# First block of two feed-forward stages: token chunk outermost, weights by blocks of 128 columns

## The chip, the cores and the metric

The kernel runs on one NeuronCore of a Trainium2 chip. The time is device microseconds of one launch; of the kernel before there are three runs. The core has five engines that each work through their own list of instructions in order and wait for each other by semaphores: TensorE (PE; its weight loads are listed as PEld), VectorE (DVE), ScalarE (ACT), GpSimd (POOL) and SyncE (SP), the last of which issues only DMAs here. GpSimd issues DMAs too.

## The reference

One decoder layer over 1088 tokens (1024 of a prompt, 64 of 8 samples), 1024 channels, in float32:

```
x = x + 0.5 * swiglu(rmsnorm(x, norm_ffn1), ffn1_w_up, ffn1_w_down)
h = rmsnorm(x, norm_mix);  q, k, v, u, g_a, g_b = split(h @ w_in)
x = x + (sigmoid(g_a) * (attention(q, k, v) @ w_attn_branch)
         + sigmoid(g_b) * (pool(u) @ w_pool_branch)) @ w_out
x = x + 0.5 * swiglu(rmsnorm(x, norm_ffn2), ffn2_w_up, ffn2_w_down)
swiglu(h, w_up, w_down): gate, up = split(h @ w_up);  (silu(gate) * up) @ w_down
```

`w_up` is 1024 x 5632 (2816 gate columns, then 2816 up columns), `w_down` 2816 x 1024. The attention is a dilated window attention in three groups, with a bias per distance and head looked up in a table; the biases are prepared at the start of the kernel.

## The kernel before

**Products.** A product is made of three matmuls in a reduced 32-bit format: each operand is split into a high part (a copy by ScalarE that rounds) and a low part (VectorE's subtraction of it), and `mm3` adds high x high, high x low and low x high in one PSUM bank (L269, L270, L271). `split` does both steps (L215 ScalarE, L216 VectorE). The normed tokens lie as `h_hi` and `h_lo` in SBUF, channels on the partitions, 8 tiles of 128 channels; the tokens are cut into three chunks of 360, 360 and 368 columns (`CH`).

**Norm.** `normed` (L330 on) spreads the tokens' factors over the partitions with a matmul (L334), multiplies on VectorE (L337), copies to `h_hi` on ScalarE (L340) and subtracts to `h_lo`: on GpSimd for every third of the 8 tiles, on VectorE for the others (L341). In the first FFN the tokens are transposed on TensorE beforehand (L465); in the second, `norm` sums the squares first and TensorE adds them up over the partitions.

**FFN.** `ffn` (L344) is called twice (L518 and L1258). It walks over 11 blocks of 256 columns (`j`). For each, `wunit` loads 256 gate or up columns as two raw tiles `wr` of 4 x 256 per partition on SyncE's queue (512 KB each), and splits them into `wh` and `wl` of 128 columns each (two of either, from pool `wp`, three buffers per name). `gate` multiplies one half of 128 columns with one chunk, 24 matmuls into a PSUM tile `psa`, and ScalarE applies silu (L385). `up` does the same for the up columns, VectorE multiplies by the silu (L392), and `split` writes `hh` and `hl`, the operands of the down product (`down`), which runs one block later. In block 0 there is no earlier block: gate and up alternate, half `f` outermost, chunk `c` inside. From block 1 on the six gate products come first, then the down product of the block before, then the six up products. `hh`, `hl` and the pieces `dh`, `dl` of `w_down` lie in the pool `fp`, which `ffn` opens on the right side of SBUF.

**What lies there before.** Two pools, `bp` and `ip`, are open on that side until just before the first `ffn` and hold the raw tokens and the tiles of the biases: the one-hot matrix `oh`, the table `tb`, and `fr`, three buffers of 4 x 448. `biases` (L430) makes four rows sets on TensorE (L438), copies each to `fr` on VectorE (L440), and has GpSimd issue two DMAs: `fr` to `f_scr` in DRAM (L441), and for three of the four sets `fr` 128 times over to `f_rep` in DRAM (L443, 512 rows of 448 values). GpSimd then builds `b_scr` by small DMAs out of `f_scr` (L497 to L506). A first write into memory that a closed pool held waits for what still uses it.

**Order.** The engines' lists are written out by a scheduler that simulates the kernel and orders each engine's instructions by it; an order in the source is a wish, not the order of the list. PSUM has four banks `psa`, and `psb` for the rest; the tiles `tmp` have eight buffers.

Of the kernel before, what the change touches and what calls it, by code (L numbers as in the profile page):

```python
# [11 lines left out]
F32 = mybir.dt.float32  # L12
F32R = mybir.dt.float32r
# [7 lines left out]
P = 128  # L21
D = 1024
KD = D // P
# [5 lines left out]
DFF = 2816  # L29
# [88 lines left out]
def body(ctx, tc, x_prompt, x_sample, c128, c512, c2048, state_pool, rel_bias_table,  # L118
# [14 lines left out]
    wp = ctx.enter_context(tc.tile_pool(name="wp", bufs=3))  # L133
# [9 lines left out]
    def psb():  # L143
        return ps.tile([P, 512], F32, tag="b", name="psb")

    def tmp():
        return tmp_pool[0].tile([P, 368], F32, tag="tmp", name="tmp", bufs=8)
# [40 lines left out]
    def load(out, in_):  # L188
        last_load[0] = nc.sync.dma_start(out=out, in_=in_)
# [5 lines left out]
    for g, w in enumerate(WIN):  # L195
        n = (w - 8) * 512
# [11 lines left out]
    def some_copies(n):  # L208
        for _ in range(min(n, len(copies))):
            o, i = copies.pop()  # L210
            with tc.issue_after(last_load[0].ins):
                nc.sync.dma_start(out=o, in_=i)

    def split(hi, lo, src):
        S.activation(hi, src, AF.Copy)  # L215
        V.tensor_tensor(out=lo, in0=src, in1=hi.bitcast(F32), op=ALU.subtract)  # L216

    def wtiles():

        return [[wp.tile([P, KD, P], F32R, tag=x, name=x) for x in ("wh", "wl")] for _ in range(2)]  # L220

    def wsplit(w, f, sl, raw):
        split(w[f][0][:, sl, :], w[f][1][:, sl, :], raw[:, :, f * P:(f + 1) * P])

    def wunit(src):
        w = wtiles()
        raws = []
        for k0 in range(0, KD, 4):
            raw = wp.tile([P, 4, 256], F32, tag="wr", name="wr", bufs=3)
            load(raw, src[k0 * P:(k0 + 4) * P].rearrange("(k p) n -> p k n", p=P))  # L230
            raws.append((raw, slice(k0, k0 + 4)))
        for f in range(2):
            for raw, sl in raws:
                wsplit(w, f, sl, raw)
        return w
# [23 lines left out]
    def taken():  # L259
        w, job = fetched.pop(0)  # L260
        il.finish(job)
        return w

    def mm3(out, pairs, us=0.0):
        n = len(pairs)
        for i, (lh, ll, rh, rl) in enumerate(pairs):
            if i and us:
                il.advance(us)
            PE.matmul(out, lh, rh, start=i == 0, stop=False)  # L269
            PE.matmul(out, lh, rl, start=False, stop=False)  # L270
            PE.matmul(out, ll, rh, start=False, stop=i == n - 1)  # L271

    def proj(w, half, c, hi, lo, ks=(0, KD)):
        if hi is h_hi:
            il.finish(norms[c])
        c0, n = CH[c]
        o = psa()[:, :n]
        wh, wl = w[half]
        mm3(o, [(wh[:, k, :], wl[:, k, :], hi[:, k, c0:c0 + n], lo[:, k, c0:c0 + n])
                for k in range(*ks)], 0.462)  # L280
        clock_after[0] += 0.462
        return o
# [3 lines left out]
    def go():  # L286
        us, clock_after[0] = clock_after[0], 0.0
        il.advance(us)
# [55 lines left out]
    def ffn(xt, w_up, w_down, ncopy, hook):  # L344
        fctx = ExitStack()
        fp = fctx.enter_context(tc.tile_pool(name="fp", bufs=1, side="right"))

        def down(j, hh, hl, last):
            raws, pcs = [], {}
            for f in range(2):  # L350
                r = fp.tile([P, D], F32, tag="dr", name="dr", bufs=2)
                load(r, w_down[(2 * j + f) * P:(2 * j + f + 1) * P, :])
                raws.append(r)
            some_copies(ncopy)
            for dq in range(4):
                for f in range(2):
                    ph = fp.tile([P, 256], F32R, tag="dh", name="dh", bufs=8)
                    pl = fp.tile([P, 256], F32R, tag="dl", name="dl", bufs=8)
                    split(ph, pl, raws[f][:, dq * 256:(dq + 1) * 256])
                    pcs[dq, f] = (ph, pl)  # L360

            def one(d, c):
                c0, n = CH[c]
                o = psb()[:, :n]
                sl = slice((d % 2) * P, (d % 2 + 1) * P)
                mm3(o, [(pcs[d // 2, f][0][:, sl], pcs[d // 2, f][1][:, sl],
                         hh[:, f, c0:c0 + n], hl[:, f, c0:c0 + n]) for f in range(2)])
                xd = xt[:, d, c0:c0 + n]
                V.scalar_tensor_tensor(out=xd, in0=o, scalar=0.5, in1=xd, op0=ALU.mult, op1=ALU.add)  # L369
                il.advance(0.92)  # L370

            if last:
                for c in range(3):
                    for d in range(KD):
                        one(d, c)
                        hook(c, d)
            else:
                for d in range(KD):
                    for c in range(3):
                        one(d, c)  # L380

        def gate(w, f, c):
            o = proj(w, f, c, h_hi, h_lo)
            t = tmp()[:, :CH[c][1]]
            S.activation(t, o, AF.Silu)  # L385
            go()
            return t

        def up(w, f, c, t, hh, hl):
            c0, n = CH[c]  # L390
            o = proj(w, f, c, h_hi, h_lo)
            V.tensor_tensor(out=t, in0=t, in1=o, op=ALU.mult)  # L392
            split(hh[:, f, c0:c0 + n], hl[:, f, c0:c0 + n], t)
            go()

        prev = None
        for j in range(11):
            wg = wunit(w_up[:, j * 256:(j + 1) * 256])
            sil = {}
            if prev is not None:  # L400
                for f in range(2):
                    for c in range(3):
                        sil[f, c] = gate(wg, f, c)
                down(*prev, False)
            wu = wunit(w_up[:, DFF + j * 256:DFF + (j + 1) * 256])
            hh = fp.tile([P, 2, T], F32R, tag="hh", name="hh")
            hl = fp.tile([P, 2, T], F32R, tag="hl", name="hl")
            if prev is None:
                for f in range(2):
                    for c in range(3):  # L410
                        up(wu, f, c, gate(wg, f, c), hh, hl)
            else:
                for f in range(2):
                    for c in range(3):
                        up(wu, f, c, sil[f, c], hh, hl)
            prev = (j, hh, hl)
        down(*prev, True)
        fctx.close()
# [93 lines left out]
    def hook1(c, d):  # L512
# [3 lines left out]
        norms[c] = il.spawn(norm(xt, c, 1))  # L516

    ffn(xt, ffn1_w_up[0], ffn1_w_down[0], 2, hook1)  # L518
    qctx = ExitStack()
    qp = qctx.enter_context(tc.tile_pool(name="qp", bufs=2, side="right"))  # L520
# [21 lines left out]
    for c, gi in [(c, gi) for i in range(2) for c in range(3) for gi in (2 * i, 2 * i + 1)]:  # L542
            c0, n = CH[c]
# [609 lines left out]
    for i in range(8):  # L1153
        w = taken()
# [25 lines left out]
    for i in range(4):  # L1180
        w = taken()
# [36 lines left out]
    for i in range(4):  # L1218
        w = taken()
# [33 lines left out]
    def hook2(c, d):  # L1253
        emit_outs()
        if d % 2:
            outs.append((c, d - 1))

    ffn(xt, ffn2_w_up[0], ffn2_w_down[0], 2, hook2)  # L1258
    emit_outs()
    some_copies(len(copies))  # L1260
# [36 lines left out]
```

## Time and profile before

| | |
|---|---|
| median of 3 runs | 2554.17 us (2551.82, 2554.17, 2554.18) |
| profiled execution, its own time | 2554.82 us |
| its span | 2553.0 us |
| TensorE busy | 2420.6 us (95%), 14820 matmuls |
| VectorE busy | 1098.7 us (43%) |
| ScalarE busy | 615.9 us (24%) |
| GpSimd busy | 179.1 us (7%) |
| TensorE's granted clock, mean | 0.968 of full |

The profile is of one execution, and all times of its rows are microseconds from the start of the span. A row of the timeline gives the start, the busy time, the engine, the line, the operation, the output and the inputs by their names (without numbers), and how many instructions it merges (x4); in brackets stands how long the engine had been idle, and what released it. TensorE is busy nearly throughout: in the 40 equal slices of 64 us that the page shows, it is below 90% in the first three only (0.7, 0.2 and 0.3).

### The profile page before, as it was taken

Reading aid. Unit: us, or ns where it says so; the run is one execution under the profiler, and the core shown is the slowest. Engines: PE = TensorE matmul, PEld = TensorE weight load, DVE = VectorE, ACT = ScalarE, POOL = GpSimd, SP = SyncE. Lnnn points to the kernel's source line nnn. Section 1 sums busy time; section 2 is a strip of 40 time slices with the busy share of each in tenths; the row PEclk is TensorE's granted clock in tenths of the full one; section 3 lists DMA queues with packets and bytes.
Section 4 is the critical chain, followed back from the end, with each engine's and each line's share of the span. In section 5 each row is a group of like instructions: output and inputs, shape, how many; then the busy total and the mean of one; then the engine's idle time right before and its main releaser. Section 6 shows DMA issues by size and latency. Waiting matters only on the chain.

```text
span 2553.0 us, 35907 instructions
## 1 busy us (share of the span) xinstructions
PE 2420.6 (95%) x14820; PEld 2366.8 (93%) x14820; DVE 1098.7 (43%) x2317; ACT 615.9 (24%) x1436; POOL 179.1 (7%) x304
## 2 busy tenths in 40 slices
PE   7239999999999989999999999998999999999999
PEld 6239999999999989989899979998999999999998
DVE  5014333333333484257668524627333333433334
ACT  4012111111111243343334222213111111111111
POOL 3020000000000040201011210002000000000001
PEclk8669999999999999999999999999999999999999
DMA  4231121122221122347565583621122221221132
GB/s 127 36 88 58 58 71 42 70 83 82 83 83 67 34 81 72 128 159 251 169 192 176 194 279 119 234 101 34 34 83 83 83 83 66 83 83 63 38 124 71
DMA packets 155475, 259.11 MB, mean 101 GB/s; under 512 B 14160, under 2 KB 124432, under 8 KB 154528
## 3 DMA queue, kind: packets, MB, share of 16 engines
q1 hardware_dynamic: 141296, 224.26, 26.6%
q0 software_dynamic: 14016, 32.56, 4.5%
q8 instruction: 116, 1.90, 0.3%
q14 instruction: 47, 0.39, 0.0%
HBM read 225.14 MB, written 76.32 MB: 118 GB/s over the span
## 4 chain that ended last, share of the span: by engine, by line
PE 83%; DMA 6%; issue 5%; DVE 3%; POOL 1%; ACT 1%; SPq 0%; POOLq 0%; DVEq 0%; ACTq 0%
PE psa L269 20%; PE psa L270 20%; PE psa L271 20%; PE psb L270 7%; PE psb L271 7%; PE psb L269 7%; DMA f_rep<-fr 2%; DMA b_scr<-f_scr 2%; DMA qb<-q_scr 1%; DMA u_scr<-us 1%; PE psb L864 1%; PE psb L730 1%; DMA wr<-in_ffn_w_up_dram 1%; DMA rt<-u_scr 0%; PE psb L1050 0%
## 5 line engine op out<-in xcount | busy, mean ns | idle before, releaser
L269 PE MATMUL psa<-h_hi,wh 128*128 128x360 f32 (+1 forms) x3216 | 1072.2, 334 | 67.2 <-DVE tmp L392 59.0
L270 PE MATMUL psa<-h_lo,wh 128*128 128x360 f32 (+1 forms) x3216 | 1070.8, 333 | 35.4 <-POOL h_lo L341 27.1
L271 PE MATMUL psa<-h_hi,wl 128*128 128x360 f32 (+1 forms) x3216 | 1065.1, 331 | 0.0
L269 PEld LDWEIGHTS psa<-h_hi,wh 128*128 128x128 f32 x3216 | 613.0, 191 | 79.3 <-DVE tmp L392 59.6
L270 PEld LDWEIGHTS psa<-h_lo,wh 128*128 128x128 f32 x3216 | 613.8, 191 | 43.2 <-POOL h_lo L341 27.4
L271 PEld LDWEIGHTS psa<-h_hi,wl 128*128 128x128 f32 x3216 | 613.4, 191 | 4.5 <-issue 3.6
L216 DVE TENSOR_TENSOR wl<-wr,wh 128x512 fp32r<-128x512 f32 (+1 forms) x284 | 185.4, 680 | 554.7 <-ACT wh L215 554.4
L369 DVE SCALAR_TENSOR_TENSOR xt<-psb,xt 128x360 f32<-128x360 f32 (+1 forms) x528 | 281.5, 533 | 261.6 <-PE psb L271 261.2
L270 PE MATMUL psb<-hl,dh 128*128 128x360 f32 (+1 forms) x1056 | 347.4, 329 | 0.0
L269 PE MATMUL psb<-hh,dh 128*128 128x360 f32 (+1 forms) x1056 | 347.3, 329 | 0.0
L271 PE MATMUL psb<-hh,dl 128*128 128x360 f32 (+1 forms) x1056 | 346.6, 328 | 0.0
L215 ACT ACTIVATE wh<-wr 128x512 fp32r<-128x512 f32 (+1 forms) x284 | 163.2, 618 | 457.7 <-PE psa L270 397.4
L269 PEld LDWEIGHTS psb<-hh,dh 128*128 128x128 f32 x1056 | 198.8, 188 | 0.3
L271 PEld LDWEIGHTS psb<-hh,dl 128*128 128x128 f32 x1056 | 198.5, 188 | 0.0
L270 PEld LDWEIGHTS psb<-hl,dh 128*128 128x128 f32 x1056 | 198.4, 188 | 0.2
L215 ACT ACTIVATE dh<-dr 128x256 fp32r<-128x256 f32 x176 | 72.3, 417 | 499.3 <-PE psb L270 486.5
L392 DVE TENSOR_TENSOR tmp<-tmp,psa 128x360 f32<-128x360 f32 x132 | 69.9, 530 | 211.2 <-PE psa L271 211.2
L215 ACT ACTIVATE hh<-tmp 128x360 fp32r<-128x360 f32 x132 | 65.6, 499 | 238.6 <-DVE tmp L392 198.3
L385 ACT ACTIVATE tmp<-psa 128x360 f32<-128x360 f32 x132 | 61.2, 466 | 233.6 <-PE psa L271 233.5
L216 DVE TENSOR_TENSOR hl<-tmp,hh 128x360 fp32r<-128x360 f32 x132 | 70.0, 532 | 76.0 <-ACT hh L215 75.9
L216 DVE TENSOR_TENSOR dl<-dr,dh 128x256 fp32r<-128x256 f32 x176 | 73.1, 420 | 24.9 <-ACT dh L215 21.9
L889 DVE TENSOR_TENSOR qb<-kt,qb 128x512 f32<-128x512 f32 x96 | 65.4, 684 | 30.9 <-DMA qb<-q_scr 30.2
(239 smaller groups left out, 1520.3 us busy)
## 6 DMA issues: line engine op xcount, KB each, us to landing
wr<-in_ffn_w_up_dram SPq DMA_DIRECT2D x88, 512.0 KB, 4.9
out_dram<-in_cache_kv_w_dram SPq DMA_DIRECT2D x32, 1020.0 KB, 9.4
qb<-q_scr SPq DMA_DIRECT2D x96, 256.0 KB, 4.6
dr<-in_ffn_w_down_dram SPq DMA_DIRECT2D x44, 512.0 KB, 4.2
wr<-in_w_in_dram SPq DMA_DIRECT2D x38, 512.0 KB, 4.7
kt<-in_cache_kv_w_dram SPq DMA_DIRECT2D x64, 256.0 KB, 4.3
vt<-in_cache_kv_w_dram SPq DMA_DIRECT2D x26, 512.0 KB, 8.6
t<-t_scr SPq DMA_DIRECT2D x16, 544.0 KB, 4.7
```

The source lines that it names most:

```text
L215: S.activation(hi, src, AF.Copy)
L216: V.tensor_tensor(out=lo, in0=src, in1=hi.bitcast(F32), op=ALU.subtract)
L269: PE.matmul(out, lh, rh, start=i == 0, stop=False)
L270: PE.matmul(out, lh, rl, start=False, stop=False)
L271: PE.matmul(out, ll, rh, start=False, stop=i == n - 1)
L369: V.scalar_tensor_tensor(out=xd, in0=o, scalar=0.5, in1=xd, op0=ALU.mult, op1=ALU.add)
L385: S.activation(t, o, AF.Silu)
L392: V.tensor_tensor(out=t, in0=t, in1=o, op=ALU.mult)
L730: PE.matmul(o[:rows, 4 * t + 2 * f:4 * t + 2 * f + 2], sqs[f][:, t * P:t * P + rows], halves, start=True, stop=True)
L864: PE.matmul(o[:, h * 64:(h + 1) * 64], pts[i][:, h * P:(h + 1) * P], vs[:, k, h * 64:(h + 1) * 64], start=i == 0, stop=i == len(kt) - 1)
L889: V.tensor_tensor(out=qb, in0=kt.to_broadcast([P, 2, 256]) if g == 0 else kt, in1=qb, op=ALU.mult))
```

## The change

Only the first block (`j` = 0) of both calls of `ffn` is edited. Its weights are now loaded by `wblock`: 128 columns in one raw tile of 8 x 128 per partition (as large as the former tile of 4 x 256, with rows of 512 bytes in DRAM in place of 1024), split in two steps into one pair `wh`, `wl`. The chunk is the outer loop and the half the inner one, so that chunk 0 goes through both halves before chunk 1 is touched. The first halves of gate and up are loaded at the start, the second ones when the loop first comes to them. Three of the four blocks lie in `wp`; the last (the up weights of the second half) lies in `fp`, beside `hh` and `hl`.

```diff
--- before.py
+++ after.py
@@ -393,21 +393,35 @@
             split(hh[:, f, c0:c0 + n], hl[:, f, c0:c0 + n], t)
             go()
 
+        def wblock(c0, pool):
+
+            w = [pool.tile([P, KD, P], F32R, tag=x, name=x) for x in ("wh", "wl")]
+            raw = wp.tile([P, KD, P], F32, tag="wr", name="wr", bufs=3)
+            load(raw, w_up[:, c0:c0 + P].rearrange("(k p) n -> p k n", p=P))
+            for k0 in range(0, KD, 4):
+                split(w[0][:, k0:k0 + 4, :], w[1][:, k0:k0 + 4, :], raw[:, k0:k0 + 4, :])
+            return w
+
         prev = None
         for j in range(11):
-            wg = wunit(w_up[:, j * 256:(j + 1) * 256])
             sil = {}
-            if prev is not None:
+            if prev is None:
+                wg, wu = [wblock(0, wp)], [wblock(DFF, wp)]
+            else:
+                wg = wunit(w_up[:, j * 256:(j + 1) * 256])
                 for f in range(2):
                     for c in range(3):
                         sil[f, c] = gate(wg, f, c)
                 down(*prev, False)
-            wu = wunit(w_up[:, DFF + j * 256:DFF + (j + 1) * 256])
+                wu = wunit(w_up[:, DFF + j * 256:DFF + (j + 1) * 256])
             hh = fp.tile([P, 2, T], F32R, tag="hh", name="hh")
             hl = fp.tile([P, 2, T], F32R, tag="hl", name="hl")
             if prev is None:
-                for f in range(2):
-                    for c in range(3):
+                for c in range(3):
+                    for f in range(2):
+                        if len(wg) == f:
+                            wg.append(wblock(P, wp))
+                            wu.append(wblock(DFF + P, fp))
                         up(wu, f, c, gate(wg, f, c), hh, hl)
             else:
                 for f in range(2):
```

The scheduler turns this into other lists. The first piece is ScalarE's list around the first write of `hh` in the first FFN (L385 silu, L340 `h_hi`, L215 `split`), of before:

```order
L385 ACTIVATE tmp<-psa 128x360
L340 ACTIVATE h_hi<-tmp 128x368 x4
L385 ACTIVATE tmp<-psa 128x360
L215 ACTIVATE wh<-wr 128x512 x2
L385 ACTIVATE tmp<-psa 128x368
L385 ACTIVATE tmp<-psa 128x360
L215 ACTIVATE wh<-wr 128x512 x2
L385 ACTIVATE tmp<-psa 128x360
L215 ACTIVATE hh<-tmp 128x360 x2
```

and of the changed kernel:

```order
L385 ACTIVATE tmp<-psa 128x360
L340 ACTIVATE h_hi<-tmp 128x368 x4
L385 ACTIVATE tmp<-psa 128x360
L215 ACTIVATE hh<-tmp 128x360
L215 ACTIVATE wh<-wr 128x512 x2
L215 ACTIVATE dh<-dr 128x256 x8
L215 ACTIVATE hh<-tmp 128x360
L385 ACTIVATE tmp<-psa 128x360
L215 ACTIVATE hh<-tmp 128x360
```

From here to the first `hh` there stood five silu activations and four weight splits; now there are two activations, and the next weight split stands behind that `hh`.

The second piece is GpSimd's list around the bias copies in the first FFN, of before:

```order
L441 DMA f_scr<-fr 4x448
L443 DMA f_rep<-fr 512x1x448
L341 TENSOR_TENSOR h_lo<-tmp,h_hi 128x368
L502 DMA b_scr<-f_scr 8x4x128 x8
L505 DMA b_scr<-f_scr 32x1x8 x4
L341 TENSOR_TENSOR h_lo<-tmp,h_hi 128x368
L441 DMA f_scr<-fr 4x448
L443 DMA f_rep<-fr 512x1x448
L441 DMA f_scr<-fr 4x448 x2
L443 DMA f_rep<-fr 512x1x448
```

and of the changed kernel, whose L455, L457, L516 and L519 are the former L441, L443, L502 and L505:

```order
L455 DMA f_scr<-fr 4x448
L457 DMA f_rep<-fr 512x1x448
L455 DMA f_scr<-fr 4x448
L457 DMA f_rep<-fr 512x1x448
L341 TENSOR_TENSOR h_lo<-tmp,h_hi 128x368
L516 DMA b_scr<-f_scr 8x4x128 x8
L519 DMA b_scr<-f_scr 32x1x8 x2
L341 TENSOR_TENSOR h_lo<-tmp,h_hi 128x368
L455 DMA f_scr<-fr 4x448
L519 DMA b_scr<-f_scr 32x1x8 x2
L455 DMA f_scr<-fr 4x448
L457 DMA f_rep<-fr 512x1x448
```

The second `f_rep` copy stood behind twelve `b_scr` copies and now stands in front of them, with one `f_scr` copy between it and the first.

The third piece is TensorE's list of the first FFN behind the last of the four bias matmuls. `psa_609` takes the up product of the second half with chunk 0, with weights `wh_574` from `fp`; `psa_637` is the gate of chunk 1. Of the changed kernel:

```order
L452 MATMUL psb_438<-oh_116,tb_115 4x448
L269 MATMUL psa_609<-h_hi_91,wh_574 128x360
L270 MATMUL psa_609<-h_lo_92,wh_574 128x360
L269 MATMUL psa_637<-h_hi_91,wh_493 128x360
L270 MATMUL psa_637<-h_lo_92,wh_493 128x360
L271 MATMUL psa_637<-h_hi_91,wl_494 128x360
```

and of before, where `psa_582` and `psa_609` are gate and up of the first half with chunk 1, both with weights from `wp`:

```order
L438 MATMUL psb_438<-oh_116,tb_115 4x448
L271 MATMUL psa_582<-h_hi_91,wl_494 128x360
L269 MATMUL psa_582<-h_hi_91,wh_493 128x360
L270 MATMUL psa_582<-h_lo_92,wh_493 128x360
L271 MATMUL psa_582<-h_hi_91,wl_494 128x360
L270 MATMUL psa_609<-h_lo_92,wh_509 128x360
```

Three products of chunk 0 are over where the changed list begins, and the fourth is spread between those of chunk 1.

The fourth piece is TensorE's list in the second FFN around the matmul that spreads chunk 1's factors (L334). Of before, where `psa_15142` is the up product of the first half with chunk 0, and `psa_15191` and `psa_15252` are gate and up of chunk 1:

```order
L269 MATMUL psa_15142<-h_hi_91,wh_15063 128x360
L270 MATMUL psa_15142<-h_lo_92,wh_15063 128x360
L271 MATMUL psa_15142<-h_hi_91,wl_15064 128x360
L334 MATMUL psb_15103<-tmp_15001,ones_78 128x360
L269 MATMUL psa_15191<-h_hi_91,wh_15047 128x360
L269 MATMUL psa_15252<-h_hi_91,wh_15063 128x360
L270 MATMUL psa_15191<-h_lo_92,wh_15047 128x360
L271 MATMUL psa_15191<-h_hi_91,wl_15048 128x360
```

and of the changed kernel, where `psa_15126` is the up product of the first half with chunk 0, and `psa_15191` is the gate of the second half with chunk 0:

```order
L269 MATMUL psa_15126<-h_hi_91,wh_15055 128x360
L270 MATMUL psa_15126<-h_lo_92,wh_15055 128x360
L271 MATMUL psa_15126<-h_hi_91,wl_15056 128x360
L334 MATMUL psb_15087<-tmp_15001,ones_78 128x360
L269 MATMUL psa_15126<-h_hi_91,wh_15055 128x360
L270 MATMUL psa_15126<-h_lo_92,wh_15055 128x360
L271 MATMUL psa_15126<-h_hi_91,wl_15056 128x360
L270 MATMUL psa_15191<-h_lo_92,wh_15175 128x360
L271 MATMUL psa_15191<-h_hi_91,wl_15176 128x360
L269 MATMUL psa_15191<-h_hi_91,wh_15175 128x360
```

Behind L334 there stood products of chunk 1; now there stand products of chunk 0.

## Rows read from the trace of the kernel before

**Rows 1.** Busy time by stretch: ends, length, busy us (instructions), clock, DMA share, GB/s

```profile
core 0: us, PE busy (x) PEld busy (x) DVE busy (x) ACT busy (x) POOL busy (x), PEclk, DMA share, GB/s
45.95:86.00 40.05, 16.96 (x95) 15.12 (x93) 5.49 (x11) 3.82 (x7) 5.93 (x9) 0.75 0.26 27
176.96:250.00 73.04, 73.00 (x426) 72.71 (x427) 33.40 (x67) 18.97 (x43) 9.03 (x17) 0.97 0.31 104
250.00:900.00 650.00, 650.00 (x3938) 650.00 (x3937) 245.41 (x482) 124.11 (x262) 2.33 (x3) 1.00 0.19 66
900.00:1700.00 800.00, 781.16 (x5003) 741.60 (x5002) 434.10 (x953) 266.31 (x700) 107.20 (x196) 0.97 0.52 170
1745.00:1750.00 5.00, 3.75 (x20) 2.87 (x18) 4.59 (x16) 1.25 (x4) 1.71 (x2) 1.00 0.00 0
1750.00:1755.00 5.00, 2.47 (x8) 2.17 (x9) 5.00 (x10) 2.65 (x6) 1.49 (x3) 0.71 0.00 0
```

**Rows 2.** Timeline of TensorE, first FFN: start, busy, engine, line, operation, tiles, [wait]

```profile
33.96 0.77 PE L334 MATMUL psb<-dg,ones 128*128 128x360 f32 x2
...
90.00 0.68 PE L270 MATMUL psa<-h_lo,wh 128*128 128x368 f32 x1 [27.09 <-POOL h_lo L341]
...
134.71 0.68 PE L269 MATMUL psa<-h_hi,wh 128*128 128x368 f32 x1 [26.31 <-DVE tmp L392]
...
176.96 0.67 PE L269 MATMUL psa<-h_hi,wh 128*128 128x360 f32 x1 [32.73 <-DVE tmp L392]
```

**Rows 3.** Timeline of GpSimd, the same stretch

```profile
45.95 1.14 POOL L443 DMA_DIRECT2D f_rep<-fr  x1
...
86.17 0.55 POOL L502 DMA_DIRECT2D b_scr<-f_scr  x1 [33.19 <-DMA f_rep<-fr]
...
88.97 0.97 POOL L341 TENSOR_TENSOR h_lo<-tmp,h_hi 128x368 fp32r<-128x368 f32 x1
...
90.42 1.13 POOL L443 DMA_DIRECT2D f_rep<-fr  x1
...
132.70 1.14 POOL L443 DMA_DIRECT2D f_rep<-fr  x1 [40.09 <-issue]
```

**Rows 4.** The tile f_rep from 25 to 180, issue to landing

```profile
DMA to landing us min/median/max: 39.9/41.1/41.8
```

**Rows 5.** Timeline of ScalarE, first FFN

```profile
174.06 1.69 ACT L215 ACTIVATE hh<-tmp 128x360 fp32r<-128x360 f32 x4 [40.20 <-DMA b_scr<-f_scr]
```

**Rows 6.** Busy time of TensorE on the tile psa until 176.9, matmuls counted

```profile
0.00:176.90 176.90, 58.89 (x312) 0.73 0.34 68
```

**Rows 7.** Timeline of TensorE, second FFN, first block

```profile
1736.16 0.33 PE L269 MATMUL psa<-h_hi,wh 128*128 128x360 f32 x1
...
1748.19 0.87 PE L334 MATMUL psb<-tmp,ones 128*128 128x360 f32 x2 [0.32 <-DVE tmp L325]
...
1765.64 0.78 PE L334 MATMUL psb<-tmp,ones 128*128 128x368 f32 x2
...
1801.84 0.33 PE L269 MATMUL psa<-h_hi,wh 128*128 128x360 f32 x1
...
1809.71 0.33 PE L269 MATMUL psa<-h_hi,wh 128*128 128x368 f32 x1
...
1813.71 0.33 PE L269 MATMUL psa<-h_hi,wh 128*128 128x360 f32 x1
```

**Rows 8.** The page's costliest groups, the weight splits on ScalarE

```profile
L215 ACT ACTIVATE wh<-wr 128x512 fp32r<-128x512 f32 (+1 forms) x284 | 163.2, 618 | 457.7 <-PE psa L270 397.4
```

**Rows 9.** The page's DMA issues, the gate and up weights

```profile
wr<-in_ffn_w_up_dram SPq DMA_DIRECT2D x88, 512.0 KB, 4.9
```

**Rows 10.** Timeline of VectorE, second FFN, first block

```profile
1747.47 0.66 DVE L325 TENSOR_SCALAR tmp<-ident,nst 128x128 f32<-128x128 f32 x3
...
1761.74 0.67 DVE L325 TENSOR_SCALAR tmp<-ident,nst 128x128 f32<-128x128 f32 x3
```

**Rows 11.** Timeline of ScalarE, second FFN, first block

```profile
1769.54 0.45 ACT L385 ACTIVATE tmp<-psa 128x360 f32<-128x360 f32 x1
```

## The prediction

> **What bounds the kernel now.** I read the busy time in stretches first. From 176.96 us to 900 us TensorE has no gap at all, and from 900 to 1700 it is busy 781 of 800 us [rows 1]. So whatever makes TensorE late in the first FFN block arrives at the end undiminished; only what the engine does in its own gaps is free. There are two stretches with gaps around the edited code, since `ffn` is called twice: the start of the kernel and the start of the second FFN.
>
> The TensorE rows of the first stretch show three long waits, 27.09, 26.31 and 32.73 us, ending at 90.00, 134.71 and 176.96 [rows 2]. The GpSimd rows explain them. Three copies of a bias row set, `f_rep`, are issued at 45.95, 90.42 and 132.70; the second is held behind a small copy that waits 33.19 us for the first, and the third stands 40.09 us in its issue although nothing else that the profile names holds it [rows 3]. Each takes 39.9 to 41.8 us to land [rows 4]. So they run one after the other, 46 to 174. ScalarE's first write of `hh` comes at 174.06, after 40.20 us of waiting, at the landing of the third copy [rows 5] (the row names the `b_scr` copies, which stand behind it on the same queue): `hh` lies where the freed pool with `fr`, the source of these copies, was. The end of the first stretch is therefore set by the DMA chain, not by TensorE.
>
> What matters is how much TensorE gets done meanwhile. Call a unit one gate or up product of one block and one token chunk, 24 matmuls. The order of before holds 13 whole units (312 matmuls) ahead of the instruction that waits until 176.96: all twelve of block 0 and the first gate of block 1 [rows 6]. That works because ScalarE's five gate activations and its weight splits stand ahead of the first `hh` write in its order. The three copies were hidden behind the twelve units, nearly entirely.
>
> In the second FFN nothing of this kind is in memory. Its first block runs from 1736.16 to 1801.84 [rows 7], and the waits are for the norm of the chunk at hand.
>
> **The change, first FFN.** It puts both weight blocks of one half beside each other, so that chunk 0 gets its four units first; the second up block's split weights go to the pool `fp`, which lies on the freed memory as `hh` does. Three things follow from the orders.
>
> (1) What stands in front of the stop. ScalarE now has two gate activations, then the first `hh` write, then the split of the fourth weight block. TensorE's order has three units (72 matmuls) ahead of the unit that needs that fourth block. Everything else is behind it on both in-order engines. So at the stop TensorE has done 3 units rather than 13, and ten are left: six with 360 columns, four with 368. Two of the first take 1801.84 to 1809.71, so 3.94 us each; one of the second 1809.71 to 1813.71, 4.00 us [rows 7]. 6 x 3.94 + 4 x 4.00 = 39.6 us, all after the stop, with TensorE the bound from there. The slow start (the granted clock averages 0.75 from 45.95 to 86.00 [rows 1]) is there before and after: TensorE is idle ahead of the restart in both.
>
> (2) When the stop ends. The norm matmul of chunk 1 (L334, 33.96 now [rows 2]) has 65 unit matmuls ahead of it rather than 48; 17 x 0.164 us (3.94 / 24) = 2.8 us later, and the norm of chunk 2 and the first `fr` with it. First copy: 45.95 + 2.8 = 48.75, landed by 88.7 (39.9 us). GpSimd now holds the second copy right behind; I take its issue as held until the first has landed, as the third was now: 89.0, landed 130.1 (41.1). A `b_scr` copy then waits for that landing, as the one at 86.17 does now, and between it and the third `f_rep` stand seven DMA issues of 0.55 us and one `h_lo` of 0.97 [rows 3]: 130.4 + 4.8 = 135.2. It lands 41.4 us later (132.70 to 174.06 now [rows 3, 5]), 176.6. The first `hh`, a quarter of 1.69 [rows 5], and the first half of a weight split, 0.62 [rows 8], follow: TensorE resumes at 177.6 against 176.96, +0.6 us. Bounds: with 39.9 for each copy 2.6 us earlier, with 41.8 for each 3.1 us later.
>
> (3) Covered work. The later `h_lo` of chunk 2 (about 131 us) is behind the stop. The loads of `w_down` and of block 1's weights: two of the latter are now issued early, since the first buffers come free by 29 us; `w_down` is asked for at the end of the stop as it is now, and five units (20 us) cover its splits. The up-weight loads have rows of 512 bytes where they had 1024. The trace has only the old form, 4.9 us median for 512 KB [rows 9]; from 0 to another 4.9 us at the start, where the first load is waited for. I take 0, nearest to the row, since the bytes are the same.
>
> First FFN: +0.6 + 39.6 = +40.2 us; with both ends of the copies and of the load, 37 to 48.
>
> **The change, second FFN.** The memory under `fp` is free by then, and the fourth weight block is split ahead of the rush. Now 288 matmuls, 8 x 3.94 + 4 x 4.00 = 47.5 us, take 65.7 us. Two units on chunk 0 end when chunk 1's norm matmul runs (1748.19); its input was ready just then (L325 at 1747.47 plus 0.66) [rows 7, 10]. With four units on chunk 0, 37 of their matmuls stand behind that norm matmul in the new order: 6.1 us of work in the time in which VectorE makes chunk 1, until 1748.6 + 6.1 = 1754.7. Three tiny sums (about 0.8) and chunk 1's two units, 7.9: 1763.4. There chunk 2's norm matmul runs, now 1765.64; VectorE has its input by 1762.4. The next unit needs a PSUM bank that ScalarE frees by an activation 3.9 us after this matmul (1769.54 now) [rows 7, 11]: 1767.3. Six units, 2 x 3.94 + 4 x 4.00 = 23.9, end the block at 1791.2, 10.6 us before 1801.84. Bounds: no wait at that bank would make it 14.5; at the other end VectorE, busy 5.00 of 5.00 us at 1750 [rows 1], lets no more work through: 0, or 2 lost if waits at half clock fall elsewhere. I take -10.6.
>
> **Between them** nothing is edited, but the scheduler's order differs in the attention stage. TensorE is idle 18.8 us of 800 there [rows 1]; a third of that either way is my bound, 0 my value.
>
> **Sum.** 2554.8 (the profiled execution, 2553.0 of it span) + 40.2 - 10.6 = 2584.4. The median of the runs shown is 0.65 below that execution: 2584.
>
> **Rivals.**
> *The copies overlap: faster.* GpSimd now issues the second copy with only one small issue between. If it need not wait, both land by about 90, the `b_scr` copy passes at 90.4, the third copy is issued at 95.5 and lands near 137; TensorE resumes near 138 instead of 177.6. That takes 39.5 off: 2545. It decides by whether the second issue waits. For it: one copy keeps the 16 DMA engines busy at 0.26, about four of them [rows 1]. Against it: the third copy stood 40.09 us in its issue with only two small issues between it and the second [rows 3], which is what is to come. The Trainium skill speaks for this rival (DMA: Bandwidth & Descriptors, Why a DMA increments its semaphore by 16 and not by 1): the number of DMA engines follows the slowest dimension, and on GpSimd's path fewer than 16 are taken consecutively from a rotating start. By that rule two such copies would sit on different engines and run together, 2545; the share of 0.26 agrees with the first half of it, the 40.09 us wait does not show the second.
> *No gain in the second FFN.* VectorE bounds that stretch whatever TensorE's order: 2554.8 + 40.2 = 2595. For it: VectorE at 4.59 to 5.00 of 5 us there [rows 1]. Against: TensorE waits at the same time at half clock, granted 0.71 in the next 5 us [rows 1], with nothing queued; the new order gives it 37 matmuls.
> *The delay is partly absorbed.* If the attention stage's gaps are waits for transfers that would have landed anyway, up to 18.8 us go: 2565. Against it: the transfers there are asked for by work that TensorE's products feed.
>
> **Chances.** Forecast 0.74; no gain in the second FFN 0.13; overlap 0.08; absorbed 0.05. For the forecast the bounds put together give 2572 to 2598. Reaching down to the absorbed case, and with the second rival's middle inside and the overlap left out: 2566 to 2600. The 0.2% that a measurement tells from no change is 5 us; the three slower cases lie outside it. Slower 0.90, same 0.02, faster 0.08.
>
> **What would show it.** In the profile after: about 128 us without a unit matmul on TensorE, from about 48 to 177; ScalarE's `hh` write ending a wait of over 120 us; `f_rep` issues near 49, 89 and 135; ten units without a gap after the restart; the second FFN's first block in about 55 us from its first matmul. I am wrong in (2) if the second issue comes at 50; in (1) if any gate activation stands before 170 beyond the first two; in the second FFN if its first block still takes over 62 us.

## The result and the profile after

The changed kernel took 2582.43 us (median of 4 runs, 2579.32 to 2585.61) against 2553.19 (4 runs); the ratio is 1.0115, 95% interval 1.0097 to 1.0133. It is slower by some 29 us, and 2584 had been forecast. The page of the profiled execution (span, busy time, then TensorE's busy tenths and granted clock in 40 slices of 64.6 us) shows where:

```profile
span 2582.7 us, 35903 instructions
...
PE 2411.5 (93%) x14820; PEld 2359.9 (91%) x14820; DVE 1100.9 (43%) x2317; ACT 617.0 (24%) x1436; POOL 179.2 (7%) x304
...
PE   5029999999999999999999999999999999999999
...
PEclk7559999999999999999999999999999999999999
```

The difference to before lies in the first slices: TensorE is busy 0.5, 0.0 and 0.2 of the first three, with the clock at 0.7, 0.5 and 0.5. Over the whole span it does the same 14820 matmuls.

TensorE's timeline in the first FFN [rows 2] has one long wait now, where it had three:

```profile
36.74 0.77 PE L334 MATMUL psb<-dg,ones 128*128 128x360 f32 x2
...
178.28 0.67 PE L269 MATMUL psa<-h_hi,wh 128*128 128x360 f32 x1 [128.40 <-DVE hl L216]
```

Chunk 1's norm matmul comes 2.8 us later (33.96 before). From the end of the last bias matmul on, 128.40 us pass in which TensorE does nothing. Counted on `psa` until 176.9 there are 72 matmuls, three units, against 312 [rows 6]; and the stretch from the restart to 260 has no gap (columns as in [rows 1], the first without tiles other than `psa`):

```profile
0.00:176.90 176.90, 14.32 (x72) 0.60 0.34 63
```

```profile
178.28:260.00 81.72, 81.72 (x486) 81.72 (x487) 25.59 (x50) 17.38 (x38) 10.86 (x21) 0.98 0.23 74
```

GpSimd's timeline of the same time [rows 3] and the copies' time to landing [rows 4]:

```profile
49.25 1.15 POOL L457 DMA_DIRECT2D f_rep<-fr  x1 [0.24 <-issue]
...
89.68 1.11 POOL L457 DMA_DIRECT2D f_rep<-fr  x1 [38.76 <-issue]
...
131.11 0.55 POOL L516 DMA_DIRECT2D b_scr<-f_scr  x1 [35.53 <-DMA f_rep<-fr]
...
135.81 1.11 POOL L457 DMA_DIRECT2D f_rep<-fr  x1
```

```profile
DMA to landing us min/median/max: 40.0/41.1/41.1
```

The second `f_rep` copy is asked for right behind the first, but its issue is held for 38.76 us, until about the time when the first has landed (what holds it the profile does not name); the third follows at 135.81. ScalarE [rows 5]:

```profile
51.75 0.47 ACT L385 ACTIVATE tmp<-psa 128x360 f32<-128x360 f32 x1 [0.18 <-DVE h_lo L341]
177.20 0.50 ACT L215 ACTIVATE hh<-tmp 128x360 fp32r<-128x360 f32 x1 [124.98 <-DMA b_scr<-f_scr]
177.61 1.13 ACT L215 ACTIVATE wh<-wr 128x512 fp32r<-128x512 f32 x2
```

The last silu activation ahead of the stop is at 51.75; then ScalarE stands 124.98 us in front of the first `hh`, and the split of the fourth weight block, which TensorE waits for, comes right behind it.

A kernel's later course is best read from one matmul that stands at the same place in TensorE's list, or one row off it, in both: L334 of chunk 0, once at the norm after the first FFN and once at that of the second. The rows give the first and last start of six; of before, then after:

```profile
L334 PE MATMUL psb<-tmp,ones x6: 465/466/473, 909.8 to 942.5; 128*128 128x360 f32 x4, 128*128 128x368 f32 x2
...
L334 PE MATMUL psb<-tmp,ones x6: 464/469/570, 1733.2 to 1766.0; 128*128 128x360 f32 x4, 128*128 128x368 f32 x2
```

```profile
L334 PE MATMUL psb<-tmp,ones x6: 466/466/472, 949.6 to 983.2; 128*128 128x360 f32 x4, 128*128 128x368 f32 x2
...
L334 PE MATMUL psb<-tmp,ones x6: 464/469/570, 1767.6 to 1801.6; 128*128 128x360 f32 x4, 128*128 128x368 f32 x2
```

They cut the span in three. The table has the same three stretches of every kernel that was run, the experiments too, each from one profiled execution:

| kernel | to the mixing norm | to the second FFN's norm | to the end | span |
|---|---|---|---|---|
| before | 909.8 | 823.4 | 819.8 | 2553.0 |
| changed | 949.6 | 818.0 | 815.1 | 2582.7 |
| fourth block elsewhere | 913.9 | 812.7 | 816.4 | 2543.0 |
| first FFN only | 949.6 | 816.1 | 819.8 | 2585.5 |
| second FFN only | 909.7 | 823.3 | 815.0 | 2548.0 |
| changed, copy from DRAM | 852.6 | 822.2 | 815.1 | 2489.9 |
| changed, `fr` kept | 903.1 | 819.6 | 815.2 | 2537.9 |
| before, copy from DRAM | 821.9 | 824.8 | 817.1 | 2463.8 |
| both mends | 818.3 | 814.5 | 816.5 | 2449.3 |
| both, copy of 128 rows | 817.7 | 814.6 | 815.1 | 2447.4 |
| changed, early table load | 951.2 | 811.8 | 812.2 | 2575.2 |

So the change costs 39.8 us in the first stretch and gives back 5.4 in the second, where nothing is edited, and 4.7 in the third. How far one execution can be trusted, the table shows in part: three kernels have the former second FFN (before, first FFN only, before with the copy from DRAM), and their third stretch takes 819.8, 819.8 and 817.1 us. So a difference of 2 to 3 us there, between single executions, may be chance. The whole time varies more: nine runs of the kernel before, taken beside the later experiments, lie between 2547.15 and 2563.57 us.

In the second stretch, the attention stage, the order in which TensorE's instructions start makes three groups, of three kernels each, the same within a group instruction for instruction (but for one pair of neighbours in "before"): before, second FFN only, and before with the copy from DRAM take 823.3 to 824.8; changed, first FFN only and early table load 811.8 to 818.0; fourth block elsewhere, both mends and the copy of 128 rows 812.7 to 814.6. So, as far as single executions can say, the 5.4 us go with TensorE's list. What in the list makes them was not tried.

In the second FFN's first block TensorE's rows [rows 7], the busy time of three stretches between them (columns as in [rows 1]), and ScalarE's rows at the first silu:

```profile
1770.51 0.49 PE L269 MATMUL psa<-h_hi,wh 128*128 128x360 f32 x2
...
1782.20 0.87 PE L334 MATMUL psb<-tmp,ones 128*128 128x360 f32 x2
...
1791.68 0.44 PE L269 MATMUL psa<-h_hi,wh 128*128 128x360 f32 x1 [1.92 <-ACT tmp L385]
...
1801.25 0.78 PE L334 MATMUL psb<-tmp,ones 128*128 128x368 f32 x2
...
1805.65 0.44 PE L269 MATMUL psa<-h_hi,wh 128*128 128x360 f32 x1 [3.13 <-ACT tmp L385]
...
1831.32 0.33 PE L269 MATMUL psa<-h_hi,wh 128*128 128x360 f32 x1
```

```profile
1782.20:1791.68 9.48, 7.56 (x47) 7.25 (x46) 9.17 (x17) 5.33 (x10) 2.91 (x3) 1.00 0.00 0
1791.68:1801.25 9.57, 9.57 (x49) 9.57 (x49) 4.79 (x19) 1.23 (x3) 1.32 (x1) 0.82 0.01 3
...
1805.65:1831.32 25.67, 25.67 (x144) 25.67 (x145) 11.38 (x21) 8.19 (x17) 1.73 (x2) 0.93 0.13 41
```

```profile
1789.86 1.28 ACT L385 ACT_TABLE_LOAD   x1 [0.52 <-DVE h_lo L341]
1791.15 0.47 ACT L385 ACTIVATE tmp<-psa 128x360 f32<-128x360 f32 x1
```

The block takes 60.8 us (1770.51 to 1831.32) where it took 65.7. In the 9.5 us behind chunk 1's norm matmul TensorE now has work, as foreseen. But then it waits 1.92 us for the first silu, because ScalarE loads its table (1.28 us) just there, and after that wait and the next one of 3.13 the granted clock is down: 0.82 and 0.93 on the mean of the two stretches that follow.

### The profile page after: what moved, and what is told of

It reads as the page before. It is cut to its first block, busy times and chain, and to the rows that moved or that the text cites. A ratio compares the mean times of both kernels' runs of the same rounds, so it can differ in the third digit from the quotient of the medians.

```text
span 2582.7 us, 35903 instructions
## 1 busy us (share of the span) xinstructions
PE 2411.5 (93%) x14820; PEld 2359.9 (91%) x14820; DVE 1100.9 (43%) x2317; ACT 617.0 (24%) x1436; POOL 179.2 (7%) x304
## 4 chain that ended last, share of the span: by engine, by line
PE 83%; DMA 7%; issue 5%; DVE 3%; POOL 1%; ACT 1%; SPq 0%; POOLq 0%; DVEq 0%; ACTq 0%
PE psa L269 20%; PE psa L270 20%; PE psa L271 20%; PE psb L270 7%; PE psb L271 7%; PE psb L269 7%; DMA f_rep<-fr 2%; DMA b_scr<-f_scr 2%; DMA qb<-q_scr 1%; DMA u_scr<-us 1%; DMA rt<-u_scr 1%; DMA wr<-in_ffn_w_up_dram 1%; PE psb L744 1%; PE psb L1064 0%; PE psb L878 0%
## 5 line engine op out<-in xcount | busy, mean ns | idle before, releaser
L215 ACT ACTIVATE wh<-wr 128x512 fp32r<-128x512 f32 (+1 forms) x284 | 162.7, 618 | 376.7 <-PE psa L270 366.8
L215 ACT ACTIVATE dh<-dr 128x256 fp32r<-128x256 f32 x176 | 72.3, 417 | 499.8 <-PE psb L270 486.5
L215 ACT ACTIVATE hh<-tmp 128x360 fp32r<-128x360 f32 x132 | 66.0, 500 | 337.1 <-DVE tmp L392 211.9
L385 ACT ACTIVATE tmp<-psa 128x360 f32<-128x360 f32 x132 | 61.6, 467 | 245.4 <-PE psa L271 245.2
L903 DVE TENSOR_TENSOR qb<-kt,qb 128x512 f32<-128x512 f32 x96 | 65.7, 686 | 28.4 <-DMA qb<-q_scr 24.6
```

The lines of the kernel that those rows point to most:

```text
L903: V.tensor_tensor(out=qb, in0=kt.to_broadcast([P, 2, 256]) if g == 0 else kt, in1=qb, op=ALU.mult))
```

## The experiments

**The place of the fourth weight block.** The block lies in the tokens' pool instead of `fp`; the order by chunks and the loads of 512-byte rows stay.

```diff
-                            wu.append(wblock(DFF + P, fp))
+                            wu.append(wblock(DFF + P, xpool))
```

> The changed kernel, with the fourth weight block (up, second half) in the long-lived pool of the tokens instead of fp, for both calls; nothing else differs. Theory (the place of this block is the cost: its split stands behind the hh write that waits for the third bias copy): ScalarE's list again has five silu activations ahead of the first hh, TensorE again gets 13 units done before the stop; the norm matmul of chunk 1 has 24 more matmuls ahead of it than before the change (86 against 62 rows), so the copies and the restart come up to 4 us later, 177 to 181; the second FFN's block keeps its gain of 4.9: 2549 us, 2543 to 2554. Rival (chunk outermost itself costs the 40 us, by the late norm of chunks 1 and 2): 2582 or more. Rival (loads with rows of 512 bytes cost part of it): above 2556, with the loss ahead of 45 us in the trace.

Measured: 2544.02 us, ratio to before 0.9957 (0.9944 to 0.997). The matmuls on `psa` until 178, ScalarE's first `hh`, and TensorE's waits:

```profile
0.00:178.00 178.00, 61.24 (x312) 0.70 0.35 65
```

```profile
178.69 1.68 ACT L215 ACTIVATE hh<-tmp 128x360 fp32r<-128x360 f32 x4 [81.48 <-DMA b_scr<-f_scr]
```

```profile
94.98 0.67 PE L270 MATMUL psa<-h_lo,wh 128*128 128x368 f32 x1 [21.26 <-POOL h_lo L341]
...
181.59 0.67 PE L269 MATMUL psa<-h_hi,wh 128*128 128x360 f32 x1 [67.33 <-DVE tmp L392]
```

The stop is still there, until 181.59, and `hh` still waits for the third copy; but 13 units are done in front of it, as before the change. Of the 39.8 us all but 4.1 are gone, and the stop itself ends 4.6 us later than before (181.59 for 176.96). So with the long copies the order by chunks and the shorter rows cost little, and the place of one block nearly everything. The time lies in the range, 5 us below its value of 2549; the attention stage, with another list, took 5.3 us less than in the changed kernel (812.7 for 818.0).

**Each half of the change alone.** A flag lets one of the two calls of `ffn` keep the former first block.

```diff
-    def ffn(xt, w_up, w_down, ncopy, hook):
+    def ffn(xt, w_up, w_down, ncopy, hook, co):
...
-            if prev is None:
+            if prev is None and co:
```

> The change in the first FFN only; the second FFN as before. TensorE's list in the attention stage is then the same as in the changed kernel. Theory (first FFN +39.7 at the mixing norm, attention stage -5.4 by its other list, second FFN -4.9 by its own edit, all read from the two traces): 2553.2 + 39.7 - 5.4 = 2587.5. Rival (the 5.4 us in the attention stage are chance of one execution, or come with the second FFN's edit): 2593. Rival of the prediction's own size for the second FFN (10.6, with the attention at nothing): also 2593.

> The change in the second FFN only; the first FFN and TensorE's list in the attention stage as before. Theory (-4.9 as the traces of before and after have it): 2548.3. By the prediction's -10.6: 2542.6. If the attention's 5.4 belongs to this edit: 2543. Rival (no gain in the second FFN): 2553.

Measured: the first FFN only, 2589.23 us, ratio to before 1.0139 (1.0119 to 1.0159), which on 2553.2 is +35.5 us, between 30 and 41; the second only, 2548.21, ratio 0.9977 (0.9965 to 0.999), so -5.9, between -2.6 and -8.9. L334 in the first FFN's kernel, then in the second's:

```profile
L334 PE MATMUL psb<-tmp,ones x6: 463/468/570, 949.6 to 985.1; 128*128 128x360 f32 x4, 128*128 128x368 f32 x2
...
L334 PE MATMUL psb<-tmp,ones x6: 464/469/570, 1765.7 to 1797.1; 128*128 128x360 f32 x4, 128*128 128x368 f32 x2
```

```profile
L334 PE MATMUL psb<-tmp,ones x6: 463/469/570, 909.7 to 944.6; 128*128 128x360 f32 x4, 128*128 128x368 f32 x2
...
L334 PE MATMUL psb<-tmp,ones x6: 464/466/473, 1733.0 to 1767.0; 128*128 128x360 f32 x4, 128*128 128x368 f32 x2
```

The parts add up: the first FFN to 949.6 with the former end of 819.8, the second to 815.0 with the former start. The attention stage again goes with TensorE's list, which the first kernel shares with the changed one (816.1 and 818.0) and the second with before (823.3 and 823.4). The prediction's 10.6 us for the second FFN is refuted, by the second kernel's time and by its rows; so is the rival of no gain there. The first kernel's time alone would still allow 2593; its rows (816.1 and 819.8) do not.

**The copy's source.** `f_rep` is copied from `f_scr`, which holds the same rows in DRAM, so that only the small copies read `fr`.

```diff
-                G.dma_start(out=f_rep[g], in_=fr.unsqueeze(1).to_broadcast([4, P, BL]))
+                src = bass.AP(tensor=f_scr.tensor, offset=f_scr.offset + g * 4 * BL,
+                              ap=[[BL, 4], [0, P], [1, BL]])
+                G.dma_start(out=f_rep[g], in_=src)
```

> The changed kernel, but f_rep is copied from f_scr in DRAM instead of from fr in SBUF, in the same shape (4 rows, 128 times over); so fr is read by the small f_scr copies alone. Theory (hh waits for the memory of fr): the first hh write comes when the last f_scr copy has landed, which is issued right behind the second f_rep, near 98 us. If copies of one queue run beside each other it lands near 100 and TensorE resumes near 101, 77 us earlier: 2505. If they run one behind the other it lands near 136, TensorE resumes near 138: 2542. Rival (hh waits for the f_rep or b_scr copies themselves, as the released wait names them): no change, 2582.

Measured: 2492.46 us, ratio 0.976 (0.9741 to 0.978), better than either number. GpSimd's issues of the second and the third copy, the time to landing of all three, and ScalarE's first `hh`:

```profile
66.06 1.11 POOL L459 DMA_DIRECT2D f_rep<-f_scr  x1
...
82.96 1.13 POOL L459 DMA_DIRECT2D f_rep<-f_scr  x1
```

```profile
DMA to landing us min/median/max: 12.2/12.2/17.9
```

```profile
78.76 0.50 ACT L215 ACTIVATE hh<-tmp 128x360 fp32r<-128x360 f32 x1 [26.96 <-DMA b_scr<-f_scr]
```

A copy out of DRAM took 12.2 us twice and 17.9 once, not 41, which no theory had. `hh` comes at 78.76, ahead of the third copy's issue at 82.96, so it can't be waiting for that one. It comes when the second copy lands (66.06 + 12.2 = 78.3), behind which the last `f_scr` copies were issued: the theory's case of copies one behind the other, at a third of the length. By this alone the first wait could still have been for the queue, since the copies changed too; hence the next one.

**`fr` kept.** The copies are those of the changed kernel, out of SBUF, but `fr` lies in a pool that stays open.

```diff
-            fr = bp.tile([4, BL], F32, tag="fr", name="fr", bufs=3)
+            fr = xpool.tile([4, BL], F32, tag="fr", name="fr", bufs=3)
```

> The changed kernel with the copies as they are (out of SBUF, about 41 us each, one behind the other), but fr in the pool of the tokens, which stays open; so hh no longer lies on memory that the copies read. Theory (hh waits for fr's memory): the first hh comes near 53 us although the third copy lands near 177; what then holds TensorE is chunk 2's h_lo on GpSimd behind the copies' issues, until about 134 us, with 8.9 of block 0's 12 units done; 213.9 - 146.6 = 67 us earlier: 2515, by 10 either way for the attention stage's list. Rival (the wait is for the queue, whatever memory hh lies on): 2582, hh near 177.

Measured: 2542.59 us, ratio 0.9952 (0.9936 to 0.9968). ScalarE's first `hh`, then TensorE's two last waits:

```profile
53.44 0.49 ACT L215 ACTIVATE hh<-tmp 128x360 fp32r<-128x360 f32 x1
```

```profile
132.45 0.68 PE L270 MATMUL psa<-h_lo,wh 128*128 128x368 f32 x1 [35.57 <-POOL h_lo L341]
...
178.37 0.67 PE L269 MATMUL psa<-h_hi,wh 128*128 128x360 f32 x1 [19.77 <-DVE tmp L392]
```

The first `hh` is written at 53.44, with the second copy issued at 88.07 and the third at 135.02: the wait was for the memory, and the queue's rival falls. But the time is 27 us above the expectation. The wait until 132.45 for chunk 2's `h_lo` was expected at 134. The one until 178.37 was not: ScalarE waits there for one of two weight loads issued from 139.95 on. Its row, and that of a like wait in the kernel before:

```profile
176.51 0.63 ACT L215 ACTIVATE wh<-wr 128x512 fp32r<-128x512 f32 x1 [32.97 <-DMA wr<-in_ffn_w_up_dram]
```

```profile
132.87 0.63 ACT L215 ACTIVATE wh<-wr 128x512 fp32r<-128x512 f32 x1 [39.76 <-DMA wr<-in_ffn_w_up_dram]
```

The issues of gate and up weights between 50 and 180 us with their median time to landing, in this kernel and in the kernel before:

```profile
wr<-in_ffn_w_up_dram SPq DMA_DIRECT2D x3, 512.0 KB, 36.5
```

```profile
wr<-in_ffn_w_up_dram SPq DMA_DIRECT2D x2, 512.0 KB, 40.9
```

The same 512 KB take 4.9 us on the whole-span median [rows 9]. These five loads on SyncE's queue were issued into an SBUF copy of `f_rep` and landed about when that copy did, 33.6 to 41.1 us after their issue. It is not the same for every load: of four loads of `w_down`, as large, in the kernel with `fr` kept, the two issued right behind the first copy landed after 4.1 and 15.2 us, two others after 24.2 and 31.5. Why they are late was not tried. The kernel before paid this too: the wait that ended at 134.71 [rows 2] follows the weight split for which ScalarE had waited 39.76 us.

**The kernel before with short copies, and both mends.** The first is the kernel before with the copy out of DRAM; the second the changed kernel with the fourth block in the tokens' pool and the copy out of DRAM; the third writes that copy as 128 rows of 4 x 448.

```diff
-                              ap=[[BL, 4], [0, P], [1, BL]])
-                G.dma_start(out=f_rep[g], in_=src)
+                              ap=[[0, P], [BL, 4], [1, BL]])
+                G.dma_start(out=f_rep[g].rearrange("a p i -> p a i"), in_=src)
```

> The kernel before, with f_rep copied out of f_scr in DRAM as in the fourth experiment (12.2 us a copy there). Theory (three waits of before go with the copies): chunk 2's last h_lo near 65 us in place of 90, TensorE then 18.4 and 9.5 us of work to the point that it reached at 176.96, so 93 us: 83 less, 2470, by 10 for the attention stage's list. Then the changed order still costs some 22 us with short copies (2492 against 2470), as its stop ends near 80 with ten units left. Rival (chunk outermost is no worse once the copies are short): 2492 or more.

> Both mends on the changed kernel: the fourth weight block in the tokens' pool, and f_rep copied out of f_scr in DRAM. Theory: the waits of 21.3 and 67.3 us that the first experiment still had go: 2542 - 89 = 2454, by 10 for the attention stage's list; faster than the kernel before with short copies by the second FFN's 3 to 5 us and by what the attention's list gives. Rival (the late norm of chunks 1 and 2 shows, once no copy hides it): 2470 or more.

> As the one before, with the f_rep copy written as 128 rows of 4 x 448 in place of 4 rows of 128 x 448 (same bytes, same DRAM source). Theory (the copy's time goes with its outermost count, 4 against 128): 3 to 5 us a copy in place of 12.2, at a DMA share above 0.6; the kernel's time is the same, 2454, as nothing waits for the copies any more. Rival (12.2 us is the price of writing 512 rows of 1792 bytes): unchanged at 12.

Measured: 2466.51 us, ratio 0.9651 (0.9631 to 0.9671); 2448.37, ratio 0.9576 (0.9552 to 0.96); 2447.48, ratio 0.9578 (0.9555 to 0.9602). In the kernel before with short copies, weight loads between 50 and 180 us are back at 4.8 us:

```profile
wr<-in_ffn_w_up_dram SPq DMA_DIRECT2D x10, 512.0 KB, 4.8
...
f_rep<-f_scr POOLq DMA_DIRECT2D x3, 896.0 KB, 12.3
```

In the kernel with both mends the first `hh` waits 6.03 us, and the row now names the small copy that reads `fr`:

```profile
71.02 1.69 ACT L215 ACTIVATE hh<-tmp 128x360 fp32r<-128x360 f32 x4 [6.03 <-DMA f_scr<-fr]
```

Short copies alone do not save the changed order: with its fourth block left in `fp` it takes 2492 us (the experiment on the copy's source) against 2467 for the kernel before, and 852.6 against 821.9 to the mixing norm. With the block elsewhere too, the order by chunks no longer loses: 818.3 us to the mixing norm, and 2448 against 2467 in all, most of it (10.3 us) in the attention stage, whose list is another. The rival of a late norm (2470 or more) falls. The copy of 128 rows took 5.4 to 9.1 us, and the time is the same. Its times to landing, then the stretch of the first copy in this kernel and, behind it, in the kernel with both mends (four rows, 12.1 us), neither with a weight load beside it:

```profile
DMA to landing us min/median/max: 5.4/8.6/9.1
```

```profile
53.00:57.50 4.50, 4.50 (x27) 4.50 (x27) 2.39 (x6) 0.47 (x1) 3.81 (x7) 0.94 0.64 228
```

```profile
53.00:64.00 11.00, 11.00 (x63) 11.00 (x62) 2.71 (x6) 0.47 (x1) 3.96 (x8) 0.89 0.29 96
```

Of 3 to 5 us only the first copy, 5.4, came near; the other two ran beside 512 KB weight loads. The rival of 12 us for writing 512 rows falls. By the Trainium skill (DMA: Bandwidth & Descriptors, Why a DMA increments its semaphore by 16 and not by 1) the number of DMA engines goes by the outermost count, 4 against 128. The shares, 0.29 for the four-row copy and 0.64 here, agree in direction. The count does not tell the two four-row copies apart: out of SBUF the share was 0.26 too [rows 1], at 27 GB/s where it is 96 here. Why the source matters so much was not tried.

**The table load.** One silu of a single column ahead of the second FFN's norm takes the load of the table out of that block; TensorE's list is the same.

```diff
+    warm = xpool.tile([P, 1], F32, name="warm")
+    S.activation(warm, xt[:, 0, 0:1], AF.Silu)
```

> The changed kernel with one silu of a single column on ScalarE ahead of the second FFN's norm, so that the table load of 1.28 us no longer stands in front of that FFN's first silu; TensorE's list is the same, instruction for instruction. Theory (that load makes TensorE wait 1.92 us and so takes part of the 10.6 us that the prediction had for this block): from chunk 0's norm matmul to the end 813.2 us in place of 815.1. Rival (VectorE's making of chunk 1 and 2 sets this stretch, and the wait only moves to the next release): 815.1. In the time of the whole kernel 2 us can't be told.

A single run: 2576.95 us beside 2552.62 of before, too little to tell from the changed kernel. TensorE's wait at the first silu, and L334 around it:

```profile
1785.80 0.43 PE L269 MATMUL psa<-h_hi,wh 128*128 128x360 f32 x1 [0.66 <-ACT tmp L385]
```

```profile
L334 PE MATMUL psb<-tmp,ones x6: 464/470/567, 1763.0 to 1794.1; 128*128 128x360 f32 x4, 128*128 128x368 f32 x2
```

The wait is 0.66 us in place of 1.92, and from 1763.0 to the end of 2575.2 it is 812.2 us in place of 815.1: 2.9 us, one more than expected. The clock accounts for the rest: chunk 1's two units, from 1785.80 to 1793.84, took 8.04 us at a granted clock of 1.00, where they had taken 9.57 at 0.82. The rival falls, as far as one execution can say; the seven other kernels with the changed second FFN took 815.0 to 816.5. (The attention stage took 811.8 with the same list on TensorE and the table load and one activation more on ScalarE, so TensorE's list alone doesn't settle that stretch.)

## Why the prediction was right, point by point

- **What bounds the kernel.** Right. The delay of the first FFN arrived at the mixing norm, 39.8 us of the 40.2 that were forecast, and the experiment with `fr` kept shows that it is the memory under `hh` that sets it.
- **(1) What stands in front of the stop: 39.6 us.** Right: 3 units against 13, ten units without a gap behind the restart; the first experiment gives ten units back, and 35.7 of the 39.8 us with them.
- **(2) When the stop ends: +0.6 us.** Right but for 0.7: 178.28 for 177.6. The copies were issued at 49.25, 89.68 and 135.81 where 48.75, 89.0 and 135.2 stood. With (1) that makes 40.9 us, of which 39.8 arrived; the 1.1 between them was not traced. The rival of overlapping copies (2545) fell by the second issue's 38.76 us. By the rule of the Trainium skill that was weighed there (DMA: Bandwidth & Descriptors, Why a DMA increments its semaphore by 16 and not by 1), GpSimd's copies on fewer than 16 engines take consecutive ones from a rotating start. That two such copies would then run side by side was the prediction's inference, and this trace does not show it.
- **(3) Covered work: 0.** Held: with the stop mended the same loads cost no visible time. What was missed is that weight loads inside a copy's time can land late; here it did not count, as no weight load was issued between 31 and 177 us.
- **Second FFN: -10.6 us.** The step that failed, in size: -4.7. The block took 60.8 us where about 55 had been named as the sign, under the 62 beyond which it called itself wrong. The work behind chunk 1's norm matmul ran as said, until 1789.03. Then came four pieces that the sum did not have: the wait of 1.92 for the silu table; chunk 1's two units in 9.57 us instead of 7.9, at a clock of 0.82; 4.40 us to the bank that frees the next unit, not 3.9; and six units in 25.67, not 23.9, at 0.93. Together 5.9. The table load stood in the trace of before too, at 1754.63, but there no wait of TensorE ended with the silu behind it. Moving it gave back 2.9 in one execution: 1.3 of the wait, 1.5 of the lower clock.
- **Between them: 0, by 6.3 either way.** -5.4, inside the bound and outside the value. The rival that this stage absorbs the delay falls: with the same list on TensorE it took 824.8 us in the kernel before with short copies, which comes to it 88 us earlier, and 823.4 in the kernel before.
- **The number.** 2584 for 2582.4 is partly luck: 5.9 too much gain and 5.4 too little cancel. The range was also narrower than its parts. At the slow end they (48, +2 and 6.3) add up to some 2610, not 2598, as the second FFN was left there at -10.6. The result did not come near that end.

## What to carry to other kernels

When a weight block is moved, look at which pool it lands in: a write into memory that a closed pool held waits for that pool's last reader, and on an engine that works in order all that stands behind the write waits too. Count what the bound engine has in its list ahead of such a stop; that count, not the length of the stop, was the price here. And a stop that other work hides is worth mending before the order around it is tuned: here shorter copies gave 88 us to the kernel before, and with one block moved as well the changed order, 29 us slower at first, came out 18 us faster than that. Of these 18 some 10 lie in the attention stage, which was not edited.

## What the hardware showed that was not expected

- The same 896 KB, 4 rows 128 times over, took 39.3 to 41.8 us out of four SBUF partitions and 12.1 to 18.0 us out of DRAM, both in four-row form; written as 128 rows out of DRAM, 5.4 to 9.1.
- Five loads of 512 KB on another queue took 33.6 to 41.1 us when they were issued into such an SBUF copy, against a median of 4.8 with the short ones; two of `w_down`, issued at the start of a copy, took 4.1 and 15.2.
- A stretch of 820 us with the same work differed by 13 us (811.8 to 824.8) between kernels in which it was not edited. It went with the order of TensorE's list: within each of three lists, three kernels lay 1.5, 1.9 and 6.2 us apart, the widest with two instructions more on ScalarE in one of them.
